# Computing the first sixteen modulation sums on TensorE instead of VectorE, and reordering the start of a two-layer encoder

## The chip, the cores and the metric

The kernel runs on one core of one Trainium2 chip. The metric is the device time of one execution in microseconds; the time given for a kernel is the median of its runs. TensorE multiplies matrices (the profile calls it PE, and its weight loads PEld), VectorE is DVE, ScalarE is ACT, GpSimd is POOL, and SP is the engine on whose queue nearly all DMAs are issued.

## The reference

Two layers of an encoder with 512 positions and 1024 channels, in float32. Each layer is modulated by a conditioning vector c. What matters here is how a layer starts:

```
c_act = silu(c)
for l in range(2):
    mod = c_act @ w_mod[l] + b_mod[l]              # 6144 sums over 1024 products
    sh1, sc1, g1, sh2, sc2, g2 = split(mod, 6)     # 1024 each
    h = rmsnorm(x, norm1[l]) * (1 + sc1) + sh1
    u = h @ w_in[l]                                # 1024 -> 1760
    o_a = mla_mixer(u_a, ...)       # dense attention, rotary tables of 32
    o_b = dilated_mixer(u_b, ...)   # windowed attention, rotary tables of 64
    o_c = s5_mixer(u_c, ...)        # state-space scan, from exp and sin of its parameters
    x = x + g1 * (concat(rmsnorm of each) @ w_out[l])
    h2 = rmsnorm(x, norm2[l]) * (1 + sc2) + sh2
    x = x + g2 * conv_ffn(h2, ...)
```

## The kernel before

The layout keeps channels on the 128 partitions: x is `xs`, eight tiles of 128 x 512. `mod` is kept as 48 columns of 128 for each layer, `modv[l]`; columns 0 to 7 are sh1, 8 to 15 are sc1. The first projection of layer 0 therefore needs columns 0 to 15 before anything else, two of them (k and 8 + k) for each tile k of h.

**Modulation.** `mod_chunk(l, j)` makes one column: it loads 128 x 1024 weights (512 KB) into a buffer `rawm` (three buffers of a pool `early` while layer 0's first projection runs) and has one VectorE instruction multiply them with `cact` and sum along the row (line 327; a second, tiny instruction of the same line reads the accumulator). `cact` is silu(c) on all partitions; `spread` makes it ahead of everything by two TensorE products from one partition and two ScalarE copies (lines 296 and 297).

**The input's norm.** `x_norm` squares the eight tiles on ScalarE (line 412), adds them on VectorE (`nacc`, line 421), sums over partitions on TensorE (`ssq`, line 391), takes the root in nine tiny VectorE instructions (`rs_yr`, `rs_tr`, lines 356 to 365) and spreads it by four transposes (`bc`, line 372). The last root instruction is called `ready`. R, the result, stays in one of two PSUM banks with the tag `ps` until the last tile of h is made.

**The first projection.** `proj(0, ...)` runs over k = 0 to 7. `make_h(k)` makes two modulation columns, then `g1` (line 771), then `normed`: `ht` on VectorE (line 440), the high part of h on ScalarE (line 442), its low part on VectorE (line 443). A weight tile of 128 x 768 is loaded and split in two halves of 384 columns: a ScalarE cast makes the high part `wh` (line 342), and GpSimd subtracts it to make the low part `wl` (line 343). For each of six output tiles TensorE makes three products (lines 348 to 350), so 8 x 18 = 144 instructions of 512 columns. `proj(1, ...)` then makes 8 x 15 = 120 more, and between them stand steps of `s5_prep`, which makes the state-space matrices on VectorE, ScalarE, GpSimd and TensorE (lines 562 to 637).

**What else stands here.** The first part of `s5_prep`, lines 500 to 555, works out the parameters (exp, sin, small powers) in 46 tiny VectorE instructions and six of ScalarE; it is called `start`, and is traced ahead of the norm. `rope_tables` makes three tables of 128 x 512 in 17 VectorE instructions and four ScalarE ones (lines 466 to 487); it is traced behind `proj(1, ...)`.

**What sets the order.** A scheduler places every engine's instructions ahead of time in a fixed order, by the order in which the program traces them. `low(name)` shifts a block in that order by the number in `PRI` (a negative one moves it forward), and `after(ins)` keeps a block's instructions of `ins`'s engine behind `ins` in that engine's order. SP's queue is in order too: a DMA that waits for its buffer holds up those behind it.

Of the kernel before, what the change touches and what calls it, by code (L numbers as in the profile page):

```python
# [24 lines left out]
PRI = {"xs": -400, "U1": 300, "ws": -200, "rs": -300, "cu": 10, "fin": 20, "glu": -30, "par": -30,  # L25
       "prep1": -20, "qk": 20, "rope": -20}
MK = 2
OWN = 6
TOGETHER = 300
DQ = (0, 3, 0, 0)  # L30
BLOCKS = ((0, 8), (8, 15), (15, 22))
EPS = 1e-6
# [23 lines left out]
for _name, _w in (  # L56
    ("ident", 128), ("ss", 12), ("fr", 6), ("nidx", 256), ("mf", 128), ("mb", 128),
    ("rz", 256), ("sel", 128), ("bias", 896),
):
    CONST[_name] = (_n, _w)  # L60
    _n += _w
# [9 lines left out]
def _constants():  # L71
    out = np.zeros((128, NCONST), np.float32)

    def put(name, a):
        o, w = CONST[name]
        out[:, o:o + w] = a

    p = np.arange(128)
    put("ident", np.eye(128))
    sel = np.zeros((128, 128))  # L80
    for j in range(32):
# [50 lines left out]
def _layout(inp):  # L132
# [3 lines left out]
    o["xT"] = a["x"][0].T.reshape(8, 128, N).transpose(1, 0, 2)  # L136
    o["c"] = a["c"].reshape(1, D)
    o["pos"] = a["positions"].reshape(1, N)
    o["const"] = _constants()
    o["wmod"] = a["w_mod"].transpose(0, 2, 1).reshape(L, 48, 128, D)  # L140
    cols = np.zeros((128, L, NCOL), f)
    rope = lambda g: np.concatenate([g[:16], g[16:], g[16:], g[:16]])
# [74 lines left out]
def program(ctx, tc, a, out):  # L217
# [41 lines left out]
    xs = keep.tile([128, KD, N], F32, name="xs")  # L259
    crow = strm.tile([128, 1024], F32, tag="raw", name="crow", bufs=3)  # L260
    S.dma_start(crow[:1], a["c"])
    nc.sync.dma_start(cols, a["cols"])
    for k in range(0, KD, 2):
        nc.sync.dma_start(xs[:, k:k + 2], a["xT"][:, k:k + 2])
    S.dma_start(cst[:, :NEARLY], a["const"][:, :NEARLY])

# [19 lines left out]


    cact = keep.tile([128, D], F32, name="cact")
    S.activation(cact[:1], crow[:1], AF.Tanh, scale=0.5)
    V.scalar_tensor_tensor(cact[:1], cact[:1], 1.0, crow[:1], add, mul)  # L290

    def spread():
        for i in range(2):
            o = ps("cb", "big")
            c = slice(i * 512, i * 512 + 512)
            T.matmul(o, K("mf")[:1], cact[:1, c], start=True, stop=True)
            S.copy(cact[:, c], o)

# [10 lines left out]

    def mod_chunk(l, j, pooled=False):  # L310
        with low("mod" if l or j >= 16 else "mod0"):
            mod_chunk_(l, j, pooled)

    def mod_chunk_(l, j, pooled=False):
        if cur["modraw"]:
            p_, nb = cur["modraw"]
            r = p_.tile([128, 1024], F32, tag="rawm", name="rawm", bufs=nb)
            nc.sync.dma_start(r, a["wmod"][l, j])
        else:
            r = raw_tile(a["wmod"][l, j], 1024)  # L320
        if pooled:
            G.tensor_tensor(r, r, cact, mul)
            acc = tiny("modacc", 1, bufs=4)
            S.activation(r, r, AF.Copy, scale=0.5, accum_out=acc)
            G.tensor_tensor(modv[l][:, j:j + 1], acc, col(l, "bmod", j), add)
        else:
            V.tensor_tensor_reduce(out=r, in0=r, in1=cact, scale=0.5, scalar=col(l, "bmod", j),  # L327
                                   op0=mul, op1=add, accum_out=modv[l][:, j:j + 1])

# [418 lines left out]
    def mixing(l, background):  # L748
# [7 lines left out]
        if l == 0:  # L756
            g1 = keep.tile([128, 8], F32, name="g_n10")
            start = startup(pst)
            with low("par"):
                next(start, None)  # L760
            *_, R = x_norm(slice(0, N), True)
            ready = cur["rs"]
            cur["H"] = [(ht(2 * k), ht(2 * k + 1)) for k in range(KD)]
        H = cur["H"]

        def make_h(k):
            with after(*[cur["ht"]] if k else ()):
                mod_chunk(0, 8 + k)
            with after(cur["ht"] if k else ready):
                mod_chunk(0, k)  # L770
            V.tensor_scalar(g1[:, k:k + 1], modv[0][:, 8 + k:9 + k], 1.0, col(0, "n1", k), op0=add, op1=mul)
            normed(R, g1, modv[0][:, 0:8], k, slice(0, N))
# [7 lines left out]
        def proj(gi, o):  # L780
# [3 lines left out]
            for k in range(KD):  # L784
# [3 lines left out]
                for i0 in range(0, nt, 3):  # L788
                    i1 = min(nt, i0 + 3)
                    wh, wl = split(r[:, i0 * 128:i1 * 128], (i1 - i0) * 128,  # L790
                                   G if (i0 == 0 or l + gi == 0) else V)
                    for i in range(i0, i1):
                        c = slice((i - i0) * 128, (i - i0) * 128 + 128)
                        mm3(o[i], (wh[:, c], wl[:, c]), H[k], k == 0, k == KD - 1)
# [86 lines left out]
        with ExitStack() as st:  # L881
            if l == 0:
                cur["modraw"] = (pool("early", "right", st), 3)
            if l:
# [16 lines left out]
        if l == 0:  # L901
# [11 lines left out]
            pst.close()  # L913
            with low("rope"):
                rope_tables()
        dil_roots(0, 32)
# [557 lines left out]
    banks("pa", cur["pst"], big=6, ps=2)  # L1474
    spread()
    open_norm()
# [33 lines left out]
```

## Time and profile before

| | before |
|---|---|
| median of 3 runs, us | 1503.74 (1500.45 to 1504.09) |
| the profiled execution, us | 1506.77 |
| its span, us | 1505.0 |
| granted TensorE clock, mean share of full speed | 0.959 |

The span runs from the first instruction to the last; 1.8 us of the profiled execution's time lie around it. The profiled execution is 3.0 us above the median. The change lies in the first 8 per cent of the span. There the stages are: up to 25.4 us the loads, the norm and the first tile of h; from 25.4 to 68.4 us the 144 products of `proj(0, ...)`; from 68.4 to 128.3 us `proj(1, ...)` with the state-space matrices and the rotary tables.

### The profile page before, as it was taken

The page shows a single profiled execution, that of the slowest core. Times are in us where ns is not written, and L with a number is a line of the kernel's source. Part 1 is how long each engine was busy: PE and PEld are TensorE (multiplying, and loading weights), DVE is VectorE, ACT ScalarE, POOL GpSimd, SP SyncE. Part 2 cuts the span into 40 slices and gives each one's busy share as a digit, 9 for nine tenths or more (in the row PEclk, how much of TensorE's full clock was granted, in tenths as well). Part 3 has the DMA queues.
Part 4 walks back from the last instruction along what each step waited for, and adds up shares of the span by engine and source line. Part 5 has one row for each costly group of instructions (what it writes and reads, how often), then busy time and mean ns, then how long its engine had stood idle before and what let it go on. Part 6 is the DMA issues. An engine that isn't in the chain of part 4 may idle for free.

```text
span 1505.0 us, 20265 instructions
## 1 busy us (share of the span) xinstructions
PE 1385.0 (92%) x7160; PEld 1116.8 (74%) x7160; DVE 1070.4 (71%) x2117; ACT 693.3 (46%) x1347; POOL 373.0 (25%) x322
## 2 busy tenths in 40 slices
PE   5879689888899999999998889898899999999998
PEld 3657556657878878887888777566698888888887
DVE  8996977865798789788656588767558663663663
ACT  4464255653454433544456334666445442442441
POOL 2566541220212152243234433323101000000000
PEclk9999888989999999999999989999899999999999
DMA  7665313203647377477336342000032333323322
GB/s 257 193 198 176 120 33 107 99 1 104 214 154 241 110 243 248 138 226 238 111 95 200 103 132 72 26 18 10 2 116 65 98 98 98 98 89 107 97 90 93
DMA packets 79111, 185.09 MB, mean 123 GB/s; under 512 B 12705, under 2 KB 37793, under 8 KB 79010
## 3 DMA queue, kind: packets, MB, share of 16 engines
q1 hardware_dynamic: 77712, 181.43, 38.2%
q10 hardware_dynamic: 1298, 2.37, 0.4%
q8 instruction: 56, 0.92, 0.3%
q14 instruction: 45, 0.37, 0.1%
HBM read 165.95 MB, written 15.73 MB: 121 GB/s over the span
## 4 chain that ended last, share of the span: by engine, by line
PE 65%; DVE 19%; DMA 4%; issue 4%; POOL 3%; ACT 3%; SPq 1%; DVEq 0%; ACTq 0%; POOLq 0%
PE up L349 9%; PE up L350 9%; PE up L348 9%; PE dn L350 5%; PE dn L349 5%; PE dn L348 5%; DVE rawm L327 3%; PE pv L1078 3%; PE pt L1060 2%; DMA rawm<-in_wmod 2%; PE wo L348 2%; PE wo L349 1%; PE wo L350 1%; PE u L349 1%; DVE wl L343 1%
## 5 line engine op out<-in xcount | busy, mean ns | idle before, releaser
L342 ACT CAST wh<-raw 128x512 fp32r<-128x512 f32 (+3 forms) x400 | 223.5, 567 | 305.8 <-PE dn L350 120.6
L348 PE MATMUL up<-t,wh 128*128 128x512 f32 (+1 forms) x736 | 279.4, 381 | 2.5 <-ACT t L442 2.2
L349 PE MATMUL up<-t,wl 128*128 128x512 f32 (+1 forms) x736 | 279.4, 381 | 2.0 <-DVE wl L343 1.9
L350 PE MATMUL up<-t,wh 128*128 128x512 f32 (+1 forms) x736 | 278.2, 381 | 1.2 <-DVE t L443 1.2
L343 DVE TENSOR_TENSOR wl<-raw,wh 128x512 fp32r<-128x512 f32 (+3 forms) x296 | 202.0, 686 | 105.7 <-ACT wh L342 105.3
L343 POOL TENSOR_TENSOR wl<-raw,wh 128x384 fp32r<-128x384 f32 (+1 forms) x104 | 135.9, 1308 | 276.5 <-ACT wh L342 268.9
L349 PEld LDWEIGHTS up<-t,wl 128*128 128x128 f32 x736 | 138.1, 188 | 31.1 <-DVE wl L343 3.7
L348 PEld LDWEIGHTS up<-t,wh 128*128 128x128 f32 x736 | 138.3, 188 | 30.0 <-ACT t L442 3.7
L350 PEld LDWEIGHTS up<-t,wh 128*128 128x128 f32 x736 | 137.3, 188 | 28.7 <-DVE t L443 2.4
L349 PE MATMUL dn<-gh,wl 128*128 128x512 f32 (+1 forms) x366 | 140.7, 386 | 2.0 <-DVE wl L343 2.0
L348 PE MATMUL dn<-gh,wh 128*128 128x512 f32 (+1 forms) x366 | 141.2, 387 | 0.0
L350 PE MATMUL dn<-gl,wh 128*128 128x512 f32 (+1 forms) x366 | 140.8, 386 | 0.0
L327 DVE CUSTOM_DVE_ANT_0 rawm<-rawm,cact,cols 128x1024 f32<-128x1024 f32 x84 | 115.4, 1376 | 15.1 <-DMA rawm<-in_wmod 15.1
L349 PE MATMUL u<-t,wl 128*128 128x512 f32 (+1 forms) x248 | 98.0, 396 | 8.3 <-POOL wl L343 4.4
L348 PE MATMUL u<-t,wh 128*128 128x512 f32 (+1 forms) x248 | 97.8, 399 | 4.8 <-ACT t L442 2.6
L350 PE MATMUL u<-t,wh 128*128 128x512 f32 (+1 forms) x248 | 95.6, 393 | 4.2 <-DVE t L443 4.0
L1056 ACT ACTIVATE P<-P,nb 128x512 f32<-128x512 f32 x96 | 69.1, 721 | 34.3 <-DVE nb L1054 29.1
L349 PEld LDWEIGHTS dn<-gh,wl 128*128 128x128 f32 x366 | 68.8, 188 | 15.9 <-DVE wl L343 2.8
L348 PEld LDWEIGHTS dn<-gh,wh 128*128 128x128 f32 x366 | 68.8, 188 | 14.4 <-ACT gh L1399 1.1
L350 PEld LDWEIGHTS dn<-gl,wh 128*128 128x128 f32 x366 | 68.5, 188 | 13.9 <-DVE gl L1400 1.3
L1060 PE MATMUL pt<-cst,P 128*128 128x128 f32 x384 | 63.4, 293 | 4.1 <-ACT P L1056 3.4
L1419 DVE SCALAR_TENSOR_TENSOR xs<-dn,modv,xs 128x512 f32<-128x512 f32 (+1 forms) x50 | 36.2, 727 | 41.3 <-PE dn L350 41.3
(441 smaller groups left out, 2784.2 us busy)
## 6 DMA issues: line engine op xcount, KB each, us to landing
raw<-in_w_up SPq DMA_DIRECT2D x88, 512.0 KB, 3.7
rawm<-in_wmod SPq DMA_DIRECT2D x84, 512.0 KB, 4.4
raw<-in_w_dn SPq DMA_DIRECT2D x32, 448.0 KB, 3.3
raw<-in_w_dn SPq DMA_DIRECT2D x16, 512.0 KB, 3.6
raw<-in_w_in SPq DMA_DIRECT2D x40, 192.0 KB, 2.6
raw<-in_wmod SPq DMA_DIRECT2D x12, 512.0 KB, 3.6
raw<-in_w_in SPq DMA_DIRECT2D x16, 320.0 KB, 3.7
s5wcp<-s5d SPq DMA_DIRECT2D x8, 640.0 KB, 5.7
```

The lines of the kernel that those rows point to most:

```text
L327: V.tensor_tensor_reduce(out=r, in0=r, in1=cact, scale=0.5, scalar=col(l, "bmod", j), op0=mul, op1=add, accum_out=modv[l][:, j:j + 1])
L342: S.copy(hi[:, :n], src)
L343: (eng or V).tensor_tensor(lo[:, :n], src, as32(hi[:, :n]), sub)
L348: T.matmul(o, wh, xh, start=first, stop=False)
L349: T.matmul(o, wl, xh, start=False, stop=False)
L350: return T.matmul(o, wh, xl, start=False, stop=last).ins
L1056: S.activation(P, P, AF.Exp, scale=-1.0, bias=nb, accum_out=sums)
L1060: T.transpose(t_ps[:, c], P[:, c], ident)
L1078: T.matmul(o[hh * 64:hh * 64 + 64], v[:, k, c0:c0 + 64], PT[hh][:, k], start=(first and k == 0), stop=(last and k == 3))
L1419: return V.scalar_tensor_tensor(xs[:, m, c], o, modv[l][:, 40 + m:41 + m], xs[:, m, c], mul, add).ins
```

## The change

Columns 0 to 15 of layer 0's modulation are no longer made by line 327. `mod_quad(q)` makes four of them (8 + 2q, 9 + 2q, 2q, 2q + 1) at once on TensorE: silu(c) now lies on partitions (`cth`, 128 x 8), each of its eight columns is repeated to 32 columns and loaded as weights, and a 128 x 512 block of the regrouped weights `wquad` streams past it. The eight products (float32, 128 rows, 32 output partitions) go to four groups of 32 output partitions, so to four column groups of the array, two products to a group. ScalarE copies the result to SBUF, and four products with a 0/1 column `pick` add the four groups and put the sums on partitions; VectorE adds the biases. The bytes loaded are the same (16 x 512 KB), in eight buffers instead of three.

The norm is traced first; the parameters and the rotary tables follow it, both behind `ready` on VectorE. `cols` is loaded behind `xs` instead of ahead of it. `spread` (now eight transposes) moves behind `proj(1, ...)`. In `proj(0, ...)` VectorE instead of GpSimd makes both halves of `wl`. For the other 80 columns only the factor 0.5 moves from the instruction into `cact`.

```diff
-PRI = {..., "rope": -20}
+PRI = {..., "rope": -20, "spread": -30}
+QUADS = tuple((8 + 2 * q, 9 + 2 * q, 2 * q, 2 * q + 1) for q in range(4))
...
-    crow = strm.tile([128, 1024], F32, tag="raw", name="crow", bufs=3)
-    S.dma_start(crow[:1], a["c"])
-    nc.sync.dma_start(cols, a["cols"])
+    ccol = keep.tile([128, KD], F32, name="ccol")
+    S.dma_start(ccol, a["c"])
     for k in range(0, KD, 2):
         nc.sync.dma_start(xs[:, k:k + 2], a["xT"][:, k:k + 2])
+    nc.sync.dma_start(cols, a["cols"])
...
+    cth = keep.tile([128, KD], F32, name="cth")
+    S.activation(cth, ccol, AF.Tanh, scale=0.5)
+    V.scalar_tensor_tensor(cth, cth, 1.0, ccol, add, mul)
+    V.tensor_scalar(cth, cth, 0.5, None, op0=mul)
     cact = keep.tile([128, D], F32, name="cact")
-    S.activation(cact[:1], crow[:1], AF.Tanh, scale=0.5)
-    V.scalar_tensor_tensor(cact[:1], cact[:1], 1.0, crow[:1], add, mul)
 
     def spread():
         for i in range(2):
-            o = ps("cb", "big")
-            c = slice(i * 512, i * 512 + 512)
-            T.matmul(o, K("mf")[:1], cact[:1, c], start=True, stop=True)
-            S.copy(cact[:, c], o)
+            o = ps("cb")
+            for k in range(4):
+                T.transpose(o[:, k * 128:k * 128 + 128], cth[:, 4 * i + k:4 * i + k + 1].to_broadcast([128, 128]), ident)
+            S.copy(cact[:, i * 512:i * 512 + 512], o)
...
+    def mod_quad(q):
+        o = ps("mq")
+        p_, nb = cur["modraw"]
+        for t in range(4):
+            r = p_.tile([128, 1024], F32, tag="rawm", name="rawm", bufs=nb)
+            nc.sync.dma_start(r, a["wquad"][q, t])
+            for k in (2 * t, 2 * t + 1):
+                T.matmul(o[k % 4 * 32:k % 4 * 32 + 32], cth[:, k:k + 1].to_broadcast([128, 32]), r[:, k % 2 * 512:k % 2 * 512 + 512],
+                         start=k < 4, stop=k >= 4)
+        row = p_.tile([128, 512], F32, tag="mrow", name="mrow")
+        S.copy(row, o)
+        o = ps("mc")
+        for j in range(4):
+            T.matmul(o[:, j:j + 1], row[:, j * 128:j * 128 + 128], K("pick"), start=j == 0, stop=j == 3)
+        for j in (0, 2):
+            d = QUADS[q][j]
+            V.tensor_tensor(modv[0][:, d:d + 2], o[:, j:j + 2], col(0, "bmod", d, 2), add)
...
             start = startup(pst)
-            with low("par"):
-                next(start, None)
             *_, R = x_norm(slice(0, N), True)
             ready = cur["rs"]
+            with after(ready), low("par"):
+                next(start, None)
+            with after(ready), low("rope"):
+                rope_tables()
...
         def make_h(k):
-            with after(*[cur["ht"]] if k else ()):
-                mod_chunk(0, 8 + k)
-            with after(cur["ht"] if k else ready):
-                mod_chunk(0, k)
-            V.tensor_scalar(g1[:, k:k + 1], modv[0][:, 8 + k:9 + k], 1.0, col(0, "n1", k), op0=add, op1=mul)
+            if k % 2 == 0:
+                mod_quad(k // 2)
+                V.scalar_tensor_tensor(g1[:, k:k + 2], modv[0][:, 8 + k:10 + k], 1.0, col(0, "n1", k, 2), add, mul)
             normed(R, g1, modv[0][:, 0:8], k, slice(0, N))
...
-                                   G if (i0 == 0 or l + gi == 0) else V)
+                                   G if i0 == 0 and l + gi else V)
...
-                cur["modraw"] = (pool("early", "right", st), 3)
+                early = pool("early", "right", st)
+                cur["modraw"] = early, 8
...
             pst.close()
-            with low("rope"):
-                rope_tables()
+            with low("spread"):
+                spread()
...
     banks("pa", cur["pst"], big=6, ps=2)
-    spread()
     open_norm()
```

## Rows read from the trace of the kernel before

**Rows 1.** The page, first part: busy time, share of the span, instructions of each engine

```profile
PE 1385.0 (92%) x7160; PEld 1116.8 (74%) x7160; DVE 1070.4 (71%) x2117; ACT 693.3 (46%) x1347; POOL 373.0 (25%) x322
```

**Rows 2.** Busy time by stage: PE, PEld, DVE, ACT, POOL, then PEclk, DMA share, GB/s

```profile
0.00:25.40 25.40, 6.76 (x16) 3.65 (x16) 18.94 (x77) 12.45 (x24) 4.91 (x11) 1.00 0.69 254
25.40:68.40 43.00, 38.74 (x146) 28.80 (x146) 41.83 (x60) 15.11 (x27) 24.00 (x20) 0.96 0.74 236
68.40:128.30 59.90, 48.70 (x252) 38.29 (x251) 47.79 (x88) 37.18 (x80) 34.12 (x32) 0.94 0.55 168
```

**Rows 3.** The chain that ended last, from 0 to 26 us: start, us, what

```profile
1.64 5.31 DMA xs<-in_xT
...
16.96 1.88 PE ssq L391 x8
...
24.67 0.73 ACT t L442
25.45 0.79 PE u L348
```

**Rows 4.** VectorE's groups from 0 to 70 us: xcount, busy us, mean ns

```profile
L327 DVE CUSTOM_DVE_ANT_0 rawm<-rawm,cact,cols 128x1024 f32<-128x1024 f32 x16 | 23.8, 1490 | 0.0
L443 DVE SCALAR_TENSOR_TENSOR t<-ht,modv,t 128x512 fp32r<-128x512 f32 x8 | 8.9, 1115 | 1.0 <-ACT t L442 1.0
L440 DVE SCALAR_TENSOR_TENSOR ht<-xs,g_n,bc 128x512 f32<-128x512 f32 x8 | 6.0, 745 | 0.2
```

**Rows 5.** Timeline of VectorE from 34 to 76 us: start, us, instruction

```profile
39.30 1.28 DVE L327 CUSTOM_DVE_ANT_0 rawm<-rawm,cact,cols 128x1024 f32<-128x1024 f32 x1
...
41.17 2.04 DVE L327 CUSTOM_DVE_ANT_0 rawm<-rawm,cact,cols 128x1024 f32<-128x1024 f32 x1
```

**Rows 6.** Groups of line 343: GpSimd's from 0 to 70 us, one of VectorE's

```profile
L343 POOL TENSOR_TENSOR wl<-raw,wh 128x384 fp32r<-128x384 f32 x17 | 21.7, 1282 | 36.4 <-ACT wh L342 36.3
...
L343 DVE TENSOR_TENSOR kl<-raw,kh 128x384 fp32r<-128x384 f32 x12 | 6.6, 553 | 7.1 <-ACT kh L342 7.0
```

**Rows 7.** Timeline of TensorE: float32 products at 6 and at 231 us

```profile
6.44 3.77 PE L296 MATMUL cb<-cact,cst 1*128 1x512 f32 x4 [6.44 <-DVE cact L290]
...
231.44 0.40 PE L350 MATMUL gg<-ycl,wh 128*128 128x512 f32 x1
231.77 1.95 PE L1078 MATMUL pv<-pt,vb 128*64 128x256 f32 x16
233.65 0.50 PE L348 MATMUL gv<-ych,wh 128*128 128x512 f32 x1
```

**Rows 8.** The chain that ended last, from 60 to 135 us: start, us, what

```profile
65.20 0.43 PE u L349
...
67.14 0.23 PE u L348
...
75.22 0.60 DVE tabA L480
...
103.79 0.60 DVE tabC L484
```

**Rows 9.** DMA rate from 0 to 26 us in 40 equal slices

```profile
GB/s 0 0 72 194 345 406 402 382 419 403 435 391 422 410 422 416 435 392 402 403 372 50 19 158 284 362 386 345 350 410 260 61 0 0 0 0 0 0 132 239
```

**Rows 10.** Timeline of VectorE: first and last instruction of the parameters, of the rotary tables

```profile
3.96 0.18 DVE L501 TENSOR_TENSOR m<-cols,dt 128x16 f32<-128x16 f32 x1
...
23.74 0.24 DVE L553 TENSOR_TENSOR gi<-t,t 128x80 f32<-128x80 f32 x1
...
70.11 0.87 DVE L470 CAST nR<-ht 128x512 f32<-128x512 int32 x1
...
103.72 0.68 DVE L484 SCALAR_TENSOR_TENSOR tabC<-tabS 128x512 f32<-128x512 f32 x1
```

**Rows 11.** Timeline: eight records of four transposes on TensorE, one bank copied on ScalarE

```profile
11.54 0.57 ACT L297 COPY cact<-cb 128x512 f32<-128x512 f32 x1
...
88.48 1.04 PE L612 MATMUL btp<-cst,bp 128*128 128x128 f32 x8
```

More of the change, by code (lines that the diff above doesn't have):

```diff
@@ L25 @@
 PRI = {"xs": -400, "U1": 300, "ws": -200, "rs": -300, "cu": 10, "fin": 20, "glu": -30, "par": -30,
-       "prep1": -20, "qk": 20, "rope": -20}
+       "prep1": -20, "qk": 20, "rope": -20, "spread": -30}
 MK = 2
@@ L56 @@
 for _name, _w in (
-    ("ident", 128), ("ss", 12), ("fr", 6), ("nidx", 256), ("mf", 128), ("mb", 128),
+    ("ident", 128), ("ss", 12), ("pick", 1), ("fr", 6), ("nidx", 256), ("mf", 128), ("mb", 128),
     ("rz", 256), ("sel", 128), ("bias", 896),
@@ L79, in _constants @@
     put("ident", np.eye(128))
+    put("pick", (p % 32 == 0).astype(np.float32)[:, None])
     sel = np.zeros((128, 128))
@@ L136, in _layout @@
     o["xT"] = a["x"][0].T.reshape(8, 128, N).transpose(1, 0, 2)
-    o["c"] = a["c"].reshape(1, D)
+    o["c"] = a["c"].reshape(8, 128).T
     o["pos"] = a["positions"].reshape(1, N)
@@ L140, in _layout @@
     o["wmod"] = a["w_mod"].transpose(0, 2, 1).reshape(L, 48, 128, D)
+    w = a["w_mod"][0].reshape(D, 48, 128)
+    o["wquad"] = np.stack([w[:, list(q)].reshape(4, 2, 128, 512).transpose(0, 2, 1, 3).reshape(4, 128, 1024)
+                           for q in QUADS])
     cols = np.zeros((128, L, NCOL), f)
@@ L308, in low, with mod_chunk, mod_chunk_ @@
         return tc.high_priority(-n) if n else ExitStack()
-    def mod_chunk(l, j, pooled=False):
+    def mod_chunk(l, j):
         with low("mod" if l or j >= 16 else "mod0"):
-            mod_chunk_(l, j, pooled)
-    def mod_chunk_(l, j, pooled=False):
+            mod_chunk_(l, j)
+    def mod_chunk_(l, j):
         if cur["modraw"]:
@@ L320, in mod_chunk_ @@
             r = raw_tile(a["wmod"][l, j], 1024)
[L321 to L328, printed above, removed]
+        V.tensor_tensor_reduce(out=r, in0=r, in1=cact, scale=1.0, scalar=col(l, "bmod", j),
+                               op0=mul, op1=add, accum_out=modv[l][:, j:j + 1])
+    def mod_quad(q):
[15 more added lines that the diff above has]
+            V.tensor_tensor(modv[0][:, d:d + 2], o[:, j:j + 2], col(0, "bmod", d, 2), add)
     def after(*ins):
```

## The prediction

> **What bounds the kernel now.** Over the whole span TensorE is busy 92 per cent and VectorE 71 [rows 1], but the change touches only the first 128 us, so I read the busy time by stage next. Up to 25.4 us TensorE hardly works (6.8 us). From 25.4 to 68.4 us VectorE is busy 41.8 of 43.0 us and TensorE 38.7; from 68.4 to 128.3 us it is VectorE 47.8 and TensorE 48.7 of 59.9, and ScalarE and GpSimd are over half full as well [rows 2]. In the middle stage the products alone would need less: one 512-column product follows the next in 0.23 us at the full clock (0.43 us at half clock) [rows 8], so 144 take 33.1 us. TensorE spends 43.0, and VectorE, with 97 per cent, sets the pace. Its groups say with what: 16 modulation sums take 23.8 us, the two steps of h 8.9 and 6.0 [rows 4].
>
> How near TensorE is to being the bound itself is the main point: only 9.9 us of the middle stage (43.0 less 33.1) can be won by any relief of VectorE, and the change puts new work on TensorE.
>
> **The start, up to the first product.** The chain runs over the landing of x (to 6.95 us), the adds, the sums over partitions (1.88 us from 16.96), the root, ht, t, and the first product stands at 25.45 us [rows 3]. After the change two lines meet at the first tile of h. The norm: `cols` no longer lies ahead of x, the adds are not mixed with parameters or with line 327, and the last pair of x lands about two blocks of 512 KB after the second. One block takes 1.3 us at the 400 GB/s of this stretch [rows 9], so about 9.6 us, less 0.8 us for the 316 KB of `cols`. Two squares and adds later it is 11 us; the sums add 1.9 us, nine small instructions at 0.17 us 1.6, the four transposes about 1.1: R at about 16 us. The first quad: x, `cols`, the early constants, the positions (256 KB, traced ahead of the quad) and four blocks are 5.0 MB, 12.6 us at 400 GB/s; the rate is up at about 2.6 us [rows 9], so the last block is there at 15.2. Two products on it (0.9 to 1.7 us by the price below), a copy (0.57 [rows 11]), four `pick` products (eight records of tiny products, 1.0 to 1.9, as `ssq` [rows 3]), three small adds (0.6), ht (0.75 [rows 4]) and t (0.73 [rows 3]) put the first product at 20 to 21.5 us. I take 21.5, a gain of **4.0 us**. The other end is VectorE's order. Parameters and tables stand ahead of h in the trace order, and `par` and `rope` move them forward still. They are 46 instructions of about 0.17 us, 7.9 us, and 17 that take 11.8 [rows 10]. From 14.6 us, when `ready` is done, they last until 34.3 if h had to stand behind all of them, so the first product would come at 35.8: a loss of 10.3. I stay near the early end because the parameters' instructions before the change depend on each other and already stand between the norm's (the stretch from 3.96 to 23.74 us holds both kinds), so later work gets in between; but I don't take the earliest value.
>
> **The middle stage.** Removed from VectorE: 23.8 us of sums [rows 4]. Added: 16 splits of 384 columns at 0.553 us [rows 6], 8.8 us, and about 3 us of small adds. GpSimd loses 16 of the 17 subtractions of 1.28 us [rows 6]. With GpSimd quiet the other VectorE work should shorten as well: the same sum takes 1.28 us at one time and 2.04 at another [rows 5], and t (line 443) 1115 ns in the mean [rows 4] against 0.75 us when short like ht. VectorE then needs for each k 2 x 0.55 + 2 x 0.75, with the small adds 3.0 us, against 18 x 0.23 = 4.1 us of products. The parameters and tables (19.7 us together) fill the rest; VectorE stays full, but no longer ahead of TensorE.
>
> Added on TensorE: 32 float32 products of 128 x 512. No row has this shape on four column groups. The upper bound is one after the other: `cb`, two float32 products of 512 columns at the low clock, took 3.77 us, so 1.9 each [rows 7], or about 0.9 at the full clock; 32 are 28 us. The nearest row is `pv`: eight float32 products on 64 output columns, to two halves of the partitions, took 1.95 us [rows 7], 0.24 each for 256 columns. One after the other they would need 4 x 256 columns at 0.23 us per 512, 0.46 each: two column groups do run together. By that row a quad's eight products of 512 columns are 8 x 0.49 = 3.9 us. If four groups run together as two do, 2.0 us. I take 2.0, since the two halves of `pv` lose nothing to each other, and 1.0 for the `pick` products, so 3.0 us a quad. The lower bound is the same 2.0 with the `pick` products hidden.
>
> How fast groups share the array is also told by the Trainium skill (TensorE: Matmul & The Clock Gate, "Measured speedup vs the span model"): three column groups gave 2.38 times, four row groups 3.07. At 3.07 the eight products would be an estimated 2.3 us instead of 2.0, 0.8 us more for three quads. Against the change speaks the other page (TensorEngine Tiling (Array Packing), "Key Properties"): changing the tiling mode drains the engine. The row shows what that is here: `pv` starts 0.33 us after the product ahead of it, where 0.23 is usual, and the next starts 0.19 us late behind its eight steps [rows 7]; by that, two changes of mode for a quad cost some 0.3 us, 1 us in all.
>
> The first quad lies ahead of the first product. The second has its buffers free from the start, and TensorE has little else to do up to 21.5 us; its data follow at some 23 us (8.3 MB with the first weight tiles), so half of it falls into the stage. Quads three and four fall in whole: 2.5 x 3.0 = 7.5 us. Their loads, 1.3 us a block, pass beside far longer product time, and the first quad's buffers are free by 17 us. The stage is 33.1 + 7.5 + 1.5 for stalls at the quads (mq, copy, mc and the adds share one bank of `ps`, R holds the other) = 42.1 us, a gain of **0.9**. Ends: 33.1 + 5.0 + 0.5, a gain of 4.4; by the price of one after the other (2.5 x 8 us + 33.1 + 1.5 = 54.6), a loss of 11.6.
>
> **The stage behind it.** The rotary tables leave it: 11.8 us of VectorE [rows 10], of which eight pieces, from the one at 75.22 to the one at 103.79 us, 5.7 us together, lie on the chain [rows 8]. What is late next are TensorE's weights: GpSimd's and VectorE's subtractions and the steps of `s5_prep`. In the middle stage before, VectorE's 41.8 us less 14 of the 16 sums (20.8) and h (14.9) leave 6 us of such steps; those now find VectorE full and may slip here. `spread` adds 16 records of transposes, 2.1 us at 1.04 for eight, and two copies of 0.57 [rows 11]; before, they lay in TensorE's idle start. Its sums are needed only far behind this stage, so it costs at most its TensorE time. I take 5.7 less 1.9 = **3.8 us** gained; the ends are 11.8 gained and 2 lost.
>
> **The sum.** 4.0 + 0.9 + 3.8 = 8.7 us. The profiled execution of 1506.8 us becomes 1498.1; it stands 3.0 us above the median, so the forecast for the median is 1495.
>
> **The rivals.**
>
> 1. *VectorE's order eats it.* The tables and parameters go ahead of h, the first product comes at up to 35.8 us, TensorE waits idle for it and does the quads meanwhile (the stage then is 33.1 + 3.0 + 1.5 = 37.6, 5.4 gained), and behind it the 3.8 us are kept: -10.3 + 5.4 + 3.8, 1 us slower; halfway, 4 us faster. 1500 to 1505. For it speaks the trace order; against it that each dependent instruction leaves room.
>
> 2. *TensorE becomes the bound, and the kernel slower.* Place: the column groups in the middle stage. If float32 products on 32 columns don't run together, a quad costs 8 us and the stage loses 11.6 us, against 7.8 won elsewhere: 4 us slower, 1508; if each quad also exposes the chain copy, pick, adds, ht, t (4 us), for three quads 1519. It decides from a quad of 5.5 us on: 2.5 x 2.5 us then use up most of the gain. Against it speaks `pv`.
>
> 3. *VectorE was the bound further than I say.* Its work up to 128.3 us falls by about 15 us net (23.8 of sums and 2.9 at line 443, if all eight of its instructions are short, against 11.8 added). If nearly all of it comes through, at the early end of the start, 13 to 20 us are won: 1484 to 1491. For it speak 97 per cent in the middle stage; against it TensorE's 33.1 us floor.
>
> 4. *The change doesn't do what it says*: the sums on TensorE wait for their loads and the first product stays at 25 us. Then 4.7 us remain, 1499; it lies within the forecast's spread.
>
> **How the numbers follow.** Forecast with its spread (1491 to 1499.5): 0.48. Third rival: 0.18. First and similar cases (1499.5 to 1508): 0.22. Second: 0.12. About 0.3 per cent, 4.5 us, is what a measurement of this kernel can tell from no change. Faster by more than that: 0.18 and nine tenths of the forecast and a part of the first rival, 0.65. Within it: 0.23. Slower: 0.12. A tenth is left out above 1508 and below 1483 each: 1483 to 1508. A gain of 4 us to 12 alone would be 1491 to 1499.
>
> **What would show it.** The first `u` product before 22 us in the chain; `mq` products of four column groups starting within 0.1 us of each other, a quad of 2 us; the 144 products within 42 us; no `tab` instructions behind the last of them, and the end of `proj(1, ...)` some 9 us earlier than 128.3. It would be wrong if `tab` or parameter instructions fill VectorE between `ready` and the first ht, if `mq` products follow each other at 0.43 us or more, or if behind 128.3 us the stages stretch by what was won before.

## The result and the profile after

The changed kernel takes 1521.78 us (median of 4 runs, 1516.21 to 1524.62) against 1502.76 us for the kernel before beside it (4 runs, 1500.45 to 1504.09): a ratio of 1.0124 with a 95 per cent interval of 1.0087 to 1.016, so 18.6 us slower (13 to 24). The forecast was 1495, within 1483 to 1508. It missed the sign and the range.

The profiled execution took 1524.62 us with a span of 1522.8, 17.8 more than the span before. The first view is the busy time of each engine over the whole span, which answers [rows 1]:

```profile
PE 1402.0 (92%) x7260; PEld 1121.9 (74%) x7260; DVE 1039.5 (68%) x2106; ACT 694.0 (46%) x1351; POOL 348.5 (23%) x306
```

VectorE did lose work, as meant; that alone says nothing of the time. The second view is the busy time by stage, with the stages cut where this kernel has them: up to the first `u` product, to the first TensorE product behind the 144, to the `bc` behind the state-space matrices (`bc` is a norm's root spread over the partitions; here the norm that follows `proj(1, ...)`; columns: window, length, busy time of PE, PEld, DVE, ACT, POOL with their instructions, granted clock, DMA share, GB/s). It answers [rows 2]:

```profile
0.00:28.50 28.50, 9.50 (x39) 4.26 (x39) 19.67 (x83) 14.46 (x27) 1.78 (x9) 0.92 0.83 311
28.50:81.10 52.60, 47.16 (x215) 32.92 (x216) 27.71 (x64) 17.97 (x32) 8.79 (x8) 0.94 0.47 156
81.10:136.50 55.40, 48.14 (x258) 38.59 (x257) 33.88 (x67) 34.61 (x77) 29.23 (x31) 0.94 0.57 176
```

In the middle stage VectorE is now half idle (27.7 of 52.6 us), TensorE is the busy one (47.2), and the stage is 9.6 us longer than before. Set against the terms of the sum (the stage behind is taken up to `bc`, which starts at 128.0 us before):

| term | forecast, us | the two profiles, us |
|---|---|---|
| start, up to the first `u` product | -4.0 | +3.0 (28.47 against 25.45) |
| middle stage | -0.9 | +9.6 (52.6 against 43.0) |
| stage behind it | -3.8 | -4.2 (55.4 against 59.6) |
| everything later | 0 | +9.3 |

The start and the middle stage are read from TensorE's timeline (start, duration, engine, line, operation, tile, count; in brackets the idle time ahead of it and what ended it). `mq` are the sums of a quad, two records for each of its eight products; `mc` are its four `pick` products:

```profile
15.89 1.11 PE L393 MATMUL bc<-cst,rs_yr 128*128 128x128 f32 x4 [2.04 <-DVE rs_yr L386]
16.93 3.64 PE L340 MATMUL mq<-rawm,cth 128*32 128x512 f32 x16
21.30 1.05 PE L346 MATMUL mc<-cst,mrow 128*128 128x1 f32 x8 [0.73 <-ACT mrow L343]
26.61 1.89 PE L340 MATMUL mq<-rawm,cth 128*32 128x512 f32 x2 [4.25 <-issue]
28.47 0.79 PE L369 MATMUL u<-t,wh 128*128 128x512 f32 x1
...
37.85 0.39 PE L371 MATMUL u<-t,wh 128*128 128x512 f32 x1
38.17 1.92 PE L340 MATMUL mq<-rawm,cth 128*32 128x512 f32 x14
40.80 1.05 PE L346 MATMUL mc<-cst,mrow 128*128 128x1 f32 x8 [0.72 <-ACT mrow L343]
42.22 1.88 PE L340 MATMUL mq<-rawm,cth 128*32 128x512 f32 x10 [0.36 <-PE mc L346]
44.03 0.50 PE L369 MATMUL u<-t,wh 128*128 128x512 f32 x1
...
52.39 1.06 PE L340 MATMUL mq<-rawm,cth 128*32 128x512 f32 x6
...
55.62 1.88 PE L340 MATMUL mq<-rawm,cth 128*32 128x512 f32 x10 [0.37 <-PE mc L346]
57.43 0.50 PE L369 MATMUL u<-t,wh 128*128 128x512 f32 x1
...
65.84 1.06 PE L340 MATMUL mq<-rawm,cth 128*32 128x512 f32 x6
67.67 1.05 PE L346 MATMUL mc<-cst,mrow 128*128 128x1 f32 x8 [0.78 <-ACT mrow L343]
71.19 0.50 PE L369 MATMUL u<-t,wh 128*128 128x512 f32 x1 [2.46 <-ACT t L463]
```

R is there at 17.0 us (forecast: about 16). The first quad's sixteen records run in one go behind it, in steps of 0.85 us where later quads have 0.43, and its `mc` ends at 22.35. Then TensorE waits. Between every two pairs of k stands a gap in the `u` products: 38.1 to 44.0 us, 52.3 to 57.4 and 65.7 to 71.2, 16.5 us in all. In each the whole chain of a quad lies open: the sums, the copy, the `mc` products, the adds, ht, t. TensorE is idle for 5.4 of the 16.5 us; in the rest it makes `mq`, in five pieces of 1.06 to 1.92 us, and three times `mc`, 1.05 us each. What held the first product is on VectorE's timeline (same columns):

```profile
15.67 0.16 DVE L386 SCALAR_TENSOR_TENSOR rs_yr<-rs_tr,rs_yr 128x4 f32<-128x4 f32 x1
15.92 0.42 DVE L491 CAST nR<-ht 128x512 f32<-128x512 int32 x1
18.64 0.68 DVE L501 SCALAR_TENSOR_TENSOR tabA<-ht,tabA 128x512 f32<-128x512 f32 x1
...
25.35 0.68 DVE L505 SCALAR_TENSOR_TENSOR tabC<-tabS 128x512 f32<-128x512 f32 x1
26.12 0.15 DVE L349 TENSOR_TENSOR modv<-mc,cols 128x2 f32<-128x2 f32 x1
26.93 0.73 DVE L461 SCALAR_TENSOR_TENSOR ht<-xs,g_n,bc 128x512 f32<-128x512 f32 x1
```

From the end of the root to 26.1 us it works through parameters and tables; the adds that wait on `mc` (ready at 22.35) stand behind them in its order.

Of the 9.3 us that come later, 4.8 lie in the stretches of the `dn` products, when the two traces are set side by side product for product (the feed-forward's second matrix, weights `wh` and `wl`, moving operands `gh` and `gl`). There are 1014 of them with 512 columns. Here is one group of them, in the last stage of the kernel: first before, then after (line, tile, count: shortest, median and longest in ns, first and last start):

```profile
L348 PE MATMUL dn<-gh,wh x56: 388/389/497, 1462.6 to 1500.2; 128*128 128x512 f32 x56
```

```profile
L369 PE MATMUL dn<-gh,wh x56: 393/394/398, 1479.5 to 1518.1; 128*128 128x512 f32 x56
```

Between the first and the last start lie 55 x 3 = 165 products: 37.6 us, 228 ns each, before and 38.6 us, 234 ns each, after. The `up` products (its first matrix) last 389 ns in both. Another 2.9 us arise near 450 us, where TensorE waits 3.0 us for a `wl` (1.7 before). Behind that wait the granted clock is 0.50 from 454.4 to 457.6 us, and eight products follow each other at up to 0.59 us; behind the shorter wait before it is 1.00. The wait takes 1.6 to 4.5 us in the fourteen traces of this study, and both ends of that range are found with the sums on TensorE, so nothing ties it to the change. The remaining 1.6 us lie scattered.

### The profile page after: what moved, and what is told of

It reads as the page before. It is cut to its first block, busy times and chain, and to the rows that moved or that the text cites. A ratio compares the mean times of both kernels' runs of the same rounds, so it can differ in the third digit from the quotient of the medians.

```text
span 1522.8 us, 20442 instructions
## 1 busy us (share of the span) xinstructions
PE 1402.0 (92%) x7260; PEld 1121.9 (74%) x7260; DVE 1039.5 (68%) x2106; ACT 694.0 (46%) x1351; POOL 348.5 (23%) x306
## 4 chain that ended last, share of the span: by engine, by line
PE 65%; DVE 13%; ACT 3%; POOL 3%; issue 3%; DMA 2%; DVEq 0%; SPq 0%; ACTq 0%; POOLq 0%
PE up L370 9%; PE up L371 9%; PE up L369 9%; PE dn L371 5%; PE dn L370 5%; PE dn L369 5%; PE pv L1100 3%; PE pt L1082 2%; PE wo L369 2%; PE wo L370 1%; PE wo L371 1%; DVE rawm L328 1%; DVE wl L364 1%; PE sc L1129 1%; PE ssq L412 1%
## 5 line engine op out<-in xcount | busy, mean ns | idle before, releaser
L364 DVE TENSOR_TENSOR wl<-raw,wh 128x512 fp32r<-128x512 f32 (+3 forms) x312 | 209.2, 673 | 126.6 <-ACT wh L363 126.3
L364 POOL TENSOR_TENSOR wl<-raw,wh 128x384 fp32r<-128x384 f32 (+1 forms) x88 | 113.9, 1296 | 251.2 <-ACT wh L363 231.4
L328 DVE CUSTOM_DVE_ANT_0 rawm<-rawm,cact,cols 128x1024 f32<-128x1024 f32 x68 | 92.4, 1360 | 14.8 <-DMA rawm<-in_wmod 14.4
```

The costliest lines, as they stand in the source:

```text
L328: V.tensor_tensor_reduce(out=r, in0=r, in1=cact, scale=1.0, scalar=col(l, "bmod", j), op0=mul, op1=add, accum_out=modv[l][:, j:j + 1])
L364: (eng or V).tensor_tensor(lo[:, :n], src, as32(hi[:, :n]), sub)
```

## The experiments

The theory from the two traces has three causes: VectorE's order at the start, the open chain of each quad, and a lengthening of `dn` that has nothing to do with the modulation. All ratios below are against the kernel before, run on the same chip, with median and 95 per cent interval.

**64 unused bytes in the kernel before.** The change adds two tiles of 32 bytes to the pool that lies ahead of the weight buffers, so by the program's allocation `wh` starts at byte 68640 of a partition instead of 68576, while `gh` stays at 188384.

```diff
+    pad = keep.tile([128, 16], F32, name="pad")
+    G.memset(pad, 0.0)
```

> The kernel before with 64 unused bytes per partition put behind xs, so that h, the weight buffers wh and wl and all else on that side lie 64 bytes further on and gh and gl stay where they were; nothing else differs. In the profile of the changed kernel the 1014 down-projection products (dn, 512 columns) follow each other every 233 ns, before every 227 ns, while the up-projection's stay at 227. Theory of the place (the distance between stationary and moving operand counts): dn goes to 233 ns here, up stays at 227, and the kernel is 6 us slower (0.4 per cent). Rival (the spacing of dn comes from what the other engines do beside it in the changed kernel): dn stays at 227 ns and the time within 0.1 per cent.

Measured: 1506.7 us against 1503.02, ratio 1.0026 (1.0008 to 1.0043), 3.9 us. The same group of `dn` products:

```profile
L350 PE MATMUL dn<-gh,wh x56: 394/394/396, 1466.4 to 1505.0; 128*128 128x512 f32 x56
```

38.6 us again. A kernel without any of the change pays this part, so it is a matter of addresses. The 6 us expected are the pitch alone, 6 ns for each of 1014 products; from start to start the `dn` products of the whole trace take 4.0 us more here and 4.7 more in the changed kernel. The interval of the ratio, 1.2 to 6.5 us, holds all of these.

**The changed kernel with the addresses of before.** Three one-column tiles share one, which frees the 64 bytes.

```diff
-    halfpi = keep.tile([128, 1], F32, name="halfpi")
+    three = keep.tile([128, 3], F32, name="three")
+    halfpi, zcol, epsc = (three[:, i:i + 1] for i in range(3))
...
-    zcol = keep.tile([128, 1], F32, name="zcol")
...
-    epsc = keep.tile([128, 1], F32, name="epsc")
```

> The changed kernel with three one-column constants put into one tile, which takes back the 64 bytes that its two new tiles take; all tiles on that side lie as in the kernel before. Theory of the place: dn products every 227 ns again, 6 us less than the changed kernel, so about 1515 (ratio to before 1.008); what remains is lost in the first 130 us: first u product at 28.5 us, the last of the 144 at 81, some 8.5 us behind the kernel before from 130 us on. Rival (the place doesn't count): 1521, dn at 233 ns.

Measured: 1518.14 us, ratio 1.0096 (1.0063 to 1.0129), 14.4 us slower than before; `dn` is back:

```profile
L368 PE MATMUL dn<-gh,wh x56: 388/389/504, 1473.1 to 1510.8; 128*128 128x512 f32 x56
```

By the medians the addresses are worth 4 of the 18.6 us from this side too; the intervals of the two ratios overlap, the `dn` rows don't. What follows builds on this kernel, so 14.4 us remain to be explained.

**Parameters and tables behind the first ht.** The order at the start: the block now stands in `make_h`, behind `normed`, is held behind the first ht on VectorE, and is shifted back instead of forward.

```diff
-            with after(ready), low("par"):
-                next(start, None)
-            with after(ready), low("rope"):
-                rope_tables()
...
+            if k == 0:
+                with after(cur["ht"]), low("par"):
+                    next(start, None)
+                with after(cur["ht"]), low("rope"):
+                    rope_tables()
...
-PRI = {..., "par": -30, ..., "rope": -20, ...}
+PRI = {..., "par": 40, ..., "rope": 150, ...}
```

> As a_place, and parameters and rotary tables stand behind the first ht on VectorE, at a later rank (par 40, rope 150 instead of -30 and -20). Theory (the first tile of h waits 3.8 us for VectorE, which makes tables between 22.4 and 26.1 us): first u product at about 24.7 us, the stages behind it 3 to 4 us earlier than in a_place, ratio to before 1.005 to 1.006. Rival (TensorE's own work between the products decides, the start is taken up by it, or the tables come too late and are paid behind 81 us): within 1 us of a_place.

Measured: 1520.08 us, ratio 1.0113 (1.0086 to 1.014), not told apart from the 1.0096 without the edit. The first product came where the theory put it, in TensorE's timeline at 24.41 us (28.60 without the edit):

```profile
21.37 1.05 PE L345 MATMUL mc<-cst,mrow 128*128 128x1 f32 x8 [0.73 <-ACT mrow L342]
24.41 0.78 PE L368 MATMUL u<-t,wh 128*128 128x512 f32 x1 [1.99 <-ACT t L462]
```

but nothing of it reached the end. The products end 6.2 us earlier (77.5 instead of 83.7), and `bc` of the stage behind comes 5 us later (142.6 instead of 137.6). The waits in that stage (engine, tile waited at, engine and tile waited for: us in total, times, longest) say what is late next:

```profile
POOL tm L650 <- DVE tmt L649: 11.4, 2, 8.9
POOL u L620 <- DVE u L621: 10.0, 10, 4.9
ACT wh L362 <- DMA raw<-in_w_in: 8.9, 2, 4.5
```

Without the edit the first of these rows reads 3.6 us, the second 5.5 and the third 0.4. VectorE's work that was put off stands ahead of the state-space matrices, and weights are loaded late as well; which of the two lengthens the stage more isn't shown. The rival had it that the start's gain is paid behind.

**Each quad one pair of k earlier.** Quad q + 1 is traced behind the first h of pair q, so that its chain has a pair's products beside it.

```diff
-            if k % 2 == 0:
-                mod_quad(k // 2)
+            if k == 0:
+                mod_quad(0)
+            if k % 2 == 0:
                 V.scalar_tensor_tensor(g1[:, k:k + 2], ...)
             normed(R, g1, modv[0][:, 0:8], k, slice(0, N))
+            if k % 2 == 0 and k < 6:
+                mod_quad(k // 2 + 1)
```

> As a_place, and each quad but the first is traced one pair of k earlier, so that its sums are made while the products of the pair ahead run; the order of tables is left. Theory (the chain mq, copy, mc, adds, ht, t stands open on TensorE between the pairs, 5.1 to 6.0 us each of which only 2.8 us are TensorE's work): the three interludes shrink by 2.3 to 3.2 us each, the last u product comes at 72 to 74 us instead of 81, and the kernel comes to within 0.2 per cent of before (1502 to 1506). Rival (column-group products and pick products are simply too much work for TensorE): the interludes stay over 4.5 us and the time within 3 us of a_place.

Measured: 1504.7 us, ratio 1.0009 (0.999 to 1.0027). This one edit gives back 13 of the 14.4 us. TensorE's timeline between the first and the second pair:

```profile
40.17 0.39 PE L370 MATMUL u<-t,wh 128*128 128x512 f32 x1
40.49 1.92 PE L339 MATMUL mq<-rawm,cth 128*32 128x512 f32 x16
42.34 0.50 PE L368 MATMUL u<-t,wh 128*128 128x512 f32 x1
42.67 0.40 PE L369 MATMUL u<-t,wl 128*128 128x512 f32 x1
42.91 0.40 PE L370 MATMUL u<-t,wh 128*128 128x512 f32 x1
43.14 0.39 PE L368 MATMUL u<-t,wh 128*128 128x512 f32 x1
43.38 0.95 PE L345 MATMUL mc<-cst,mrow 128*128 128x1 f32 x8
44.18 0.49 PE L369 MATMUL u<-t,wl 128*128 128x512 f32 x1
```

The sixteen records run in one piece (granted clock 1.00), the copy hides behind four products, and a quad costs TensorE about 1.9 + 0.8 us. The windows show the other side of it:

```profile
30.20:71.00 40.80, 40.80 (x206) 31.21 (x202) 28.78 (x62) 18.99 (x37) 8.71 (x10) 1.00 0.55 175
```

TensorE is busy 40.8 of 40.8 us: with the chain hidden it is itself the bound of this stage, 2.2 us shorter than before, and the first product, behind the second quad, comes 4.8 us later.

**The sums back on VectorE.** The changed kernel, addresses as before, with `mod_chunk` making the sixteen columns again (eight buffers, `spread` ahead); norm first, parameters and tables behind it, `wl` on VectorE as in the change.

```diff
-            if k % 2 == 0:
-                mod_quad(k // 2)
-                V.scalar_tensor_tensor(g1[:, k:k + 2], ...)
+            with after(*[cur["ht"]] if k else ()):
+                mod_chunk(0, 8 + k)
+            with after(cur["ht"] if k else ready):
+                mod_chunk(0, k)
+            V.tensor_scalar(g1[:, k:k + 1], ...)
```

> The kernel after, addresses as before, but with the sixteen sums on VectorE again (one instruction for each of 16 columns, eight load buffers, spread ahead as before); the norm first, parameters and tables behind it, and the halves of wl on VectorE all stay as in the change. It shows what the reordering does alone. If the place of the sums (TensorE with its open chain) is the whole loss, this comes back to the time before, about 1503 to 1506, with the products ending near 68. If the reordering costs as well (VectorE has 23.8 us of sums, 14.9 of h, 8.8 of wl between the first and the last product, 47.5 against 41.8 before, and the first product waits for tables and parameters until about 30), the products end near 78, and the time is 1510 to 1518.

Measured: 1507.19 us against 1501.31, ratio 1.0036 (1.0017 to 1.0055): 5.4 us, between the two expectations. All of the change but the sums (order, loads, `wl` on VectorE) costs this by itself; putting the sums on TensorE as the change does costs 9 more. The windows:

```profile
0.00:31.50 31.50, 4.95 (x21) 4.10 (x21) 21.46 (x83) 14.51 (x28) 2.67 (x10) 1.00 0.77 286
31.50:71.80 40.30, 37.39 (x144) 28.36 (x145) 40.30 (x85) 14.11 (x26) 5.59 (x5) 1.00 0.58 186
```

The first product is 6.0 us late, behind tables and parameters. The middle stage, with VectorE busy every microsecond, takes 40.3 us, no more than with the sums on TensorE and early. With GpSimd busy 5.6 of 40.3 us here and 24.0 of 43.0 before, a sum takes 1273 ns in the mean of this stage (1490 in [rows 4]) and t 790 (1115), so part of the 8.8 us of `wl` comes back. Beyond 71.8 us the stage behind takes 60.5, 0.9 more than before, though the tables have left it.

**Early quads, and parameters and tables behind the first ht,** with the shifts of the change (par -30, rope -20), and with the large ones (par 40, rope 150): the edits of the third and the fourth experiment together.

> The kernel after, addresses as before, each quad but the first traced one pair of k earlier, and parameters and tables placed behind the first ht on VectorE with their two shifts (par -30, rope -20) kept. If the open chain of a quad and VectorE's order at the start are two separate losses, both go: the first u product stands near 24.4 us (without the second it was 30.2), the 144 products again take about 41 us and end near 65.5, bc of the stage behind comes near 120 (125.8 with quads early alone), and the time is about 1499. If what VectorE puts off at the start is paid back behind, as it was with quads late, the products end near 65.5 all the same, but bc comes at 125 to 131 and the time is 1504 to 1510.

> As the run before it, but parameters and tables shifted further back (par 40, rope 150), as in the run that put them behind the first ht with the quads late. The first product near 24.4 us again, the 144 products 41 us or a little less. If the 11 us that the stage behind lost there came from these shifts, it loses them here too: bc near 131 and a time of about 1509, some 10 us above the run with the small shifts. If they came from the late quads alone, both runs are equal within 2 us.

Measured: 1505.05 us, ratio 1.002 (1.0 to 1.004), and 1510.75 us, ratio 1.0056 (1.0035 to 1.0077). The large shifts cost 5.7 us by themselves, where some 10 were expected (`bc` at 133.2 against 126.3). But the first product stood at 29.7 and 29.2 us, not at 24.4: both theories had left something out.

**R in SBUF,** on top of early quads with the tables behind the first ht and the small shifts. The guess was the bank that R holds.

```diff
-            *_, R = x_norm(slice(0, N), True)
+            *_, R_ = x_norm(slice(0, N), True)
+            R = cur["nt"].tile([128, N], F32, tag="Rs", name="Rs")
+            S.copy(R, R_)
```

> The kernel after, addresses as before, quads traced one pair earlier, parameters and tables behind the first ht (shifts as in the change), and R copied once by ScalarE to SBUF, so that both ps banks are free for mq and mc. With R holding one bank, the second quad could not start before the first quad's mc was read, and the first u product stood at 29 to 30 us in all three kernels with early quads. If the bank was what held it, the second quad's sixteen records now run in TensorE's idle time between about 21 and 24 us, the first u product comes at 24.5 to 25.5, the products end near 66, bc comes near 121, and the time is about 1499, 5 below the kernel with early quads alone. If something else holds the first product (the landing of the second quad or of the first weight tile), it stays at 28 to 30 and the time within 2 us of 1505.

Measured: 1505.17 us, ratio 1.0014 (0.9993 to 1.0034), and the first product at 29.82 us. The bank was not it. TensorE's timeline and then ScalarE's:

```profile
21.96 1.92 PE L339 MATMUL mq<-rawm,cth 128*32 128x512 f32 x16
28.10 1.86 PE L345 MATMUL mc<-cst,mrow 128*128 128x1 f32 x8 [4.21 <-ACT mrow L342]
29.82 1.20 PE L368 MATMUL u<-t,wh 128*128 128x512 f32 x2
```

```profile
24.37 1.28 ACT L534 ACT_TABLE_LOAD   x1
26.52 0.22 ACT L534 ACTIVATE sn<-th 128x16 f32<-128x16 f32 x1 [0.87 <-DVE th L532]
27.26 0.31 ACT L535 ACTIVATE cs<-n,three 128x16 f32<-128x16 f32 x1 [0.53 <-DVE n L533]
27.48 0.57 ACT L342 COPY mrow<-mq 128x512 f32<-128x512 f32 x1
27.94 0.51 ACT L362 CAST wh<-raw 128x384 fp32r<-128x384 f32 x1
```

The second quad is summed by 23.9 us, but its copy, and the first `wh`, stand in ScalarE's order behind two 16-column steps of the parameters, which wait for VectorE. The order of a third engine decided.

**Parameters and tables behind the second quad on ScalarE too.** As the last kernel, with the block of parameters and tables placed behind the second ht and the second quad's copy, and smaller shifts.

```diff
-        S.copy(row, o)
+        cur["mrow"] = S.copy(row, o).ins
...
+            if k == 1:
+                held = (cur["ht"], cur["mrow"])
+                with after(*held), low("par"):
+                    next(start, None)
+                with after(*held), low("rope"):
+                    rope_tables()
...
-PRI = {..., "par": -30, ..., "rope": -20, ...}
+PRI = {..., "par": -10, ..., "rope": 0, ...}
```

> As the run with R in SBUF, but parameters and tables placed behind the second ht on VectorE and behind the second quad's copy on ScalarE, with their shifts reduced (par -10, rope 0). In the run with R in SBUF the second quad's sixteen records ran from 22 to 24 us in TensorE's idle time, but ScalarE stood in order behind the parameters' steps, which wait for VectorE, so that the copy of mq was made at 27.5 us, the first wh at 27.9 and the first u product came at 29.8. If ScalarE's order is what still held the first product, it now comes at 25 to 26 us, the products end near 66, and bc of the stage behind near 120 to 122: a time of 1499 to 1501, 3 to 5 below before. If what VectorE puts off is paid back behind, as in the two runs with the large shifts, bc comes at 126 or later and the time is 1504 to 1508.

Measured: 1503.77 us against 1501.77, ratio 1.0018 (0.9995 to 1.004). The first product came at 26.55 us, 3.3 earlier, as it should if ScalarE's order held it; the edit also puts VectorE's steps further back, so the proof is the rows above and this time together. The windows:

```profile
0.00:26.60 26.60, 10.56 (x61) 5.50 (x61) 10.49 (x37) 10.18 (x20) 0.37 (x7) 1.00 0.95 368
26.60:71.60 45.00, 41.70 (x192) 30.51 (x192) 40.55 (x116) 23.45 (x45) 10.63 (x11) 0.96 0.55 174
```

What was put off now fills VectorE in the middle stage (40.6 us against 28.8 with early quads alone), which grows from 40.8 to 45.0 us; 1.4 of the 45.0 are a wait behind the last of the 144 products. `bc` comes at 123.3 us. In five executions with the order of before (the kernel itself and four padded ones) it comes between 124.6 and 128.0, and in the medians nothing of the difference is left. No version with the sums on TensorE beat the kernel before.

**What distance counts.** In the kernel before, `gh` and `gl` start a multiple of 1024 bytes away from `wh` and `wl` (188384 less 68576 is 117 x 1024), and so do the `t` tiles of the `up` products. Pads of 128, 1024 and 256 bytes instead of 64:

> The kernel before with 128 unused bytes a partition in the long-lived pool instead of 64. If what lengthens the dn products (227 ns each before, 233 with 64 bytes) is where the operands lie to each other within 128 bytes, they are back at 227 and the time equals the time before within 1.5 us. If any move does it, or one away from the old place, they stay at 233 or grow, and the time is 3 to 5 us longer.

> The kernel before with 1024 unused bytes in the long-lived pool. In the kernel before the weights wh, wl and the moving operands gh, gl of the dn products start a multiple of 1024 bytes apart (and wh and t of the up products too); with 64 and 128 unused bytes they did not, and the dn products took 232 to 234 ns instead of 227. If it is this distance that counts, 1024 bytes put it back: 227 ns, and the time of before within 1.5 us. If any move of the left pools away from their place does it, 232 to 234 ns again, and 4 to 5 us longer.

> The same with 256 unused bytes. If the distance has to be a multiple of 1024 (or of 512) bytes, the dn products take 232 to 234 ns; if a multiple of 256 is enough, 227.

Measured: 128 bytes 1506.07 us, ratio 1.0029 (1.0011 to 1.0048); 1024 bytes 1502.16 us, ratio 0.9996 (0.9977 to 1.0015); 256 bytes 1502.78 us in a single run. The group of `dn` products with 128, with 1024 and with 256 bytes:

```profile
L350 PE MATMUL dn<-gh,wh x56: 390/393/405, 1463.3 to 1501.6; 128*128 128x512 f32 x56
```

```profile
L350 PE MATMUL dn<-gh,wh x56: 388/389/499, 1458.5 to 1496.1; 128*128 128x512 f32 x56
```

```profile
L350 PE MATMUL dn<-gh,wh x56: 388/389/501, 1458.6 to 1496.2; 128*128 128x512 f32 x56
```

38.3, 37.6 and 37.6 us: with 64 and 128 bytes 232 to 234 ns a product, with 0, 256 and 1024 bytes 228. Any move would have lengthened all of them, so that reading falls; a distance that is a multiple of 256 bytes fits all five kernels. The weights' own address isn't it: the `up` products read the same `wh` and `wl`, which move by the same bytes, but their `t` tiles move along, and they keep 389 ns and a start every 227. Why the distance counts was not found.

## Why the prediction was wrong

**The bound: right.** TensorE near its own bound in the middle stage was named as the main point, and with early quads it is busy 40.8 of 40.8 us. The VectorE work that was to shorten beside a quiet GpSimd did so: the eight instructions of t went from 1115 ns to 792.

**The stage behind: the size right, the cause not shown.** It gave 4.2 us for the 3.8 of the sum, which were the tables leaving it less `spread`. With the sums on VectorE the tables left it too, `spread` did not come in, and it took 0.9 us more. In the changed kernel VectorE had half of a longer middle stage to work ahead in and was busy 33.9 us in this one (47.8 before, 42.0 with the sums on VectorE). So the agreement is in part luck.

**The price of the sums on TensorE: right.** A quad's eight products in one piece take 1.92 us at the full clock (granted 1.00); the sum took 2.0, by two halves of `pv` that lose nothing to each other [rows 7]. Four records start within 0.02 us of each other, and the next four 0.43 us later. One after the other at the price of `cb` would be an estimated 7.5 us. The Trainium skill (TensorE: Matmul & The Clock Gate, "Measured speedup vs the span model") has 3.07 in its row of four tiles, four row groups, an estimated 2.4 us here; the measured 1.92 is less. The Trainium skill (TensorEngine Tiling (Array Packing), "Key Properties") says that a change of mode drains TensorE; what the trace has for it is 0.1 us ahead of the quad, 0.32 us from start to start at 40.17 where 0.23 is usual. The 0.33 us behind the quad, at 42.34, are no sign of the mode: the product behind `mc`, which uses all columns, at 44.18, takes 0.33 too. The prediction put both sides of `pv` down to the mode; its sum held no term for it.

**The stalls at the quads: the step that failed first.** The sum had 2.5 quads at 3.0 us and 1.5 us "for stalls at the quads", 9.0 us. The trace has 16.5 us of gaps, 11.1 of quad work where 7.5 were forecast and 5.4 of idle time where 1.5 were, and some 3 us more in products that follow each other at 0.43 us and more instead of 0.23, behind waits (28.5 to 30.8 and 71.9 to 75.2 us, granted clock 0.50 in both). The prediction had listed the chain itself, in the second rival: "if each quad also exposes the chain copy, pick, adds, ht, t (4 us), for three quads 1519". It tied this to quads of 8 us and so gave it little weight. The two are independent: a whole quad is cheap, and the chain lay open all the same, because `make_h` traces a quad directly ahead of the h that needs it and one bank of `ps` takes `mq` and `mc` in turn. It also split the sums: 14 and 10 records in one gap take 1.92 and 1.88 us, as much each as 16. Tracing each quad one pair earlier takes 13 us off, in one edit, with the sums still on TensorE. That is the main cause, shown.

**The start: wrong by 7 us.** 21.5 us was forecast for the first product and 28.47 came. Two terms make it up, and the kernel with parameters and tables behind the first ht tells them apart: 24.41. So 2.9 us lie in the first quad itself. The forecast had its last block at 15.2 us and let two products wait for it (0.9 to 1.7 us); the block landed at 17.2 (issued at 7.2, 10.0 us to landing), and all sixteen records stand behind `bc` in TensorE's order and take 3.64 us, in steps of 0.85. The other 4.1 us are VectorE's order. What failed there is "I stay near the early end because the parameters' instructions before the change depend on each other": the order is fixed ahead of time, the adds were placed behind tables, and they wait for these however long `mc` has been ready. The first rival had that mechanism, at up to 10.3 us. And it isn't won by moving the tables: they come back in the stage behind (the kernels with the large shifts) or in the middle stage (the last one). With the sums on VectorE the change without them costs 5.4 us.

**The addresses: not thought of.** 4 us of the 18.6 come from two tiles of 32 bytes. The prediction went through instructions, queues and waits, and not through what the new tiles shift.

By ratios: 4 us for the addresses, 5 for all else but the sums, 9 for the sums as placed. The last two are a split of 14.4 us by one run, the 9 being what is left, and they aren't independent: with quads early and the order of the change kept, 1.4 us of the 14.4 remain (-1.5 to 4.1). What stays open: kernels with early quads and small shifts have `bc` 2 to 5 us earlier in their profiles than the profile of before, and medians 1 to 3 us above; executions differ by as much.

## What to carry to other kernels

What a step moved to another engine is worth depends on what hides its chain: write out the chain from the load to the consumer, and ask which other work stands beside each link of it in every engine's order; where the answer is none, start it one round earlier before anything else is tuned. A freed engine gives little when the next bound lies 2 us away (43.0 against 40.8 us here), and work put off is still owed in the stage that takes it. After any change of tiles compare the addresses of large operands as well as the instructions.

## What the runs showed of the hardware

A 512-column product took 232 to 234 ns instead of 228 when its weights and its moving operand started 64 or 128 bytes off a multiple of 256 bytes apart, in five kernels that differ by nothing else in these products (one of them run once): 0.3 per cent of the whole kernel. The `up` products, whose two operands moved together by the same bytes, kept 227 ns. The Trainium skill (SBUF — State Buffer, "Operand start alignment") asks of an operand's start only that it be a multiple of its element size, and says that its runs timed nothing; no figure for speed stands there.

Four float32 products with 128 rows, 32 columns each, ran side by side in four column groups: 16 records in four steps of 0.43 us at the full clock. In the first quad, whose steps are slower, four records took 0.85 us, and so did one record of `cb` alone in the kernel before.

With GpSimd busy 5.6 of 40.3 us instead of 24.0 of 43.0, VectorE's sum over 128 x 1024 took 1273 ns in the mean instead of 1490, and t 790 instead of 1115.
